# Interleaving the first two chunks of three projections, with a later split of the rows they read

## The chip, the cores and the metric

The kernel runs on one core of a Trainium2 chip. The metric is device time in microseconds of one execution. Five engines of the core work from their own instruction streams and wait for each other through semaphores: TensorE (PE, matmuls; its weight loads are listed as PEld), VectorE (DVE), ScalarE (ACT), GpSimd (POOL) and SyncE (SP, which here only issues loads). DMA queues move data beside them.

## The reference

Two layers of a decoder trunk over 256 tokens of width 2048, batch 1. What matters here is the frame around the mixers, cut to:

```python
for i in range(DEPTH):                       # DEPTH = 2
    hn = rmsnorm(h, e_norm[j] if i % 2 == 0 else o_norm[j])
    ...                                      # u = hn @ w_in; mixer (HGRN2 + RG-LRU, or mLSTM)
    mix = y @ w_out                          # output projection, 2048 x 2048
    h = h + mix
    pl = rmsnorm(p[i].astype(h.dtype) @ ple_w[i], ple_norm[i])
    h = h + jax.nn.sigmoid(h @ ple_gate_w[i]) * pl     # the gate, 2048 x 2048
return rmsnorm(h, final_norm)
```

So after each output projection the gate needs the whole new `h` as its contraction, and after the first gate the second layer's input projections (queries and keys, values `v`, output gate, `z`) need the whole `h` again.

## The kernel before

Every product is in float32, taken as three products of a high and a low part (`whi`, `wlo` of the weights, two halves of a tile `ahl` of the activations). The weights stream from memory: `load_weights` (L116 on) loads tiles of 128x1024 (`raw`), ACT casts the high part (L130) and DVE subtracts it for the low part (L131). `whi` and `wlo` have four buffers each, `raw` five, and a call of `load_weights` takes two of each.

`project_tok` (L190 on) makes a chunk: 512 output columns for 256 tokens, in two PSUM accumulators `mm`, one for each half of the tokens. It goes through four quarters of the contraction. A quarter loads its weights and issues 24 matmuls: for each token half and each of four 128-row steps, one matmul each at L205, L206 and L207. Midway in a quarter it calls `pump`, which moves every waiting side job (a Python generator in a "lane") by one step. A job's step places its instructions at that point of the program, behind the last cast and the last matmul recorded; the casts have a higher priority. The framework's scheduler then orders each engine's stream by these places, priorities and its own estimates. Every engine runs its stream in order.

The activations of a projection are needed with features on the partitions, but an output projection or a gate leaves tokens there. `to_features` (L353 on) turns one chunk round: DVE transposes blocks of 32 (L358), POOL writes the tile `w` to memory (`dfe`, `dfg` or `dfo`, L485 in `across`) and reads it back in four pieces as `r` (L488); after three steps of waiting, ACT and DVE split `r` into the `ahl` tiles (L374 and L376, or L366 and `split_act`, L145 and L146, where a gain is applied). Call the whole a hop. In the first gate, `more` then issues the gate sums (L907, on PE) two steps later, on the same `r`.

`out_proj` makes four chunks, adds each to the hidden state (L397) and starts its hop (lane "fe" in the first layer, "fo" in the second). `ple_gate`, the first gate, makes four chunks from those rows; each ends in a tanh (L410), two DVE operations (L411, L412), a square sum (L263) and a new hop (lane "fg"). The values of the second layer (`ov`) are four chunks from the "fg" rows. The last gate (`g1`, L1139 on) is three chunks from the "fo" rows, then two half chunks in another form (L1156 to L1158).

The first chunk of each of these three projections gets `before = ready(act, lane)`: ahead of quarter kq it steps the lane's job until chunk kq's rows are in `act`. So quarter 4 of a projection's first chunk reads what the last chunk before it has only just produced.

Of the kernel before, what the change touches and what calls it, by code (L numbers as in the profile page):

```python
# [11 lines left out]
F32 = mybir.dt.float32  # L12
# [7 lines left out]
P = 128  # L20
T = 256
D = 2048
KT = D // P
# [20 lines left out]
def trunk(ctx: ExitStack, tc: tile.TileContext, a, out):  # L44
    nc = tc.nc
    v, s, gp, te, sy = nc.vector, nc.scalar, nc.gpsimd, nc.tensor, nc.sync
# [6 lines left out]
    pm = ctx.enter_context(tc.tile_pool(name="pm", bufs=3, space=PSUM))  # L53
    px = ctx.enter_context(tc.tile_pool(name="px", bufs=3, space=PSUM))
# [6 lines left out]
    last = {}  # L61
# [12 lines left out]
    def pump():  # L74
        with ExitStack() as behind:
            for ins in last.values():
                behind.enter_context(tc.issue_after(ins))
            for lane in list(lanes):
                step(lane)
# [36 lines left out]
    def load_weights(src, pieces=1, queues=(sy,)):  # L116
        parts = []
        for hf in range(2):
            raw = wp.tile([P, 1024], F32, name="raw", tag="raw", bufs=5)
            hi = wp.tile([P, 1024], F32R, name="whi", tag="whi")  # L120
            lo = wp.tile([P, 1024], F32R, name="wlo", tag="wlo")
            n = 1024 // pieces
            for c in range(0, 1024, n):
                r, h, l = (x[:, c:c + n] for x in (raw, hi, lo))
                queues[(hf * 1024 + c) // n % len(queues)].dma_start(out=r, in_=src[:, hf * 1024 + c:hf * 1024 + c + n])
                with ExitStack() as order:
                    order.enter_context(tc.high_priority(offset=400))
                    if pieces > 1:
                        order.enter_context(tc.issue_after(last["split"]))
                    last["act"] = s.copy(h, r).ins  # L130
                    last["dve"] = v.tensor_tensor(out=l, in0=r, in1=h.bitcast(F32), op=ALU.subtract).ins  # L131
            parts.append((hi, lo))
            pieces = 1
        return parts
# [52 lines left out]
    def tokens(x, k, hf):  # L187
        return x[:, k, hf * P:(hf + 1) * P]

    def project_tok(w, j, act, before=None):  # L190

        ps = [pm.tile([P, 512], F32, name="mm", tag="mm") for _ in range(2)]
        for kq in range(4):
            if before is not None:
                before(kq)
            parts = load_weights(w[4 * j + kq])
            for hf in range(2):
                for kk in range(4):
                    k = kq * 4 + kk
                    hi, lo = parts[kk // 2]  # L200
                    c = (kk % 2) * 512
                    ah, al, _ = act[k // 2]
                    xh, xl = (tokens(x, k % 2, hf) for x in (ah, al))
                    wh, wl = hi[:, c:c + 512], lo[:, c:c + 512]
                    te.matmul(ps[hf], xh, wh, start=(k == 0), stop=False)  # L205
                    te.matmul(ps[hf], xh, wl, start=False, stop=False)  # L206
                    last["pe"] = te.matmul(ps[hf], xl, wh, start=False, stop=(k == KT - 1)).ins  # L207
                if hf == 0:
                    pump()
        return ps  # L210

    def newton(y, t, r, yh):
        v.tensor_scalar(t.bitcast(I32), y.bitcast(I32), 1, None, op0=ALU.logical_shift_right)
# [139 lines left out]
    def to_features(h, c, act, gain, name, more=None):  # L353

        w = room("w")
        w5 = w.rearrange("p (j c h t) -> p h c j t", j=4, c=4, h=2)
        for hf in range(2):
            v.transpose(w5[:, hf], h[:, hf].rearrange("p (c j q) -> p c j q", c=4, j=4))  # L358
        r = room("r")
        yield from across(w, r, f"d{name}{c}")  # L360
        r5 = r.rearrange("p (i c h t) -> p c h i t", i=4, c=4, h=2)
        for b in range(2):
            if gain:
                x = tp.tile([P, 512], F32, name="xr", tag="hn", bufs=3)
                for k in range(2):
                    s.activation(x[:, k * T:(k + 1) * T].rearrange("p (h i t) -> p h i t", h=2, i=4), r5[:, 2 * b + k],  # L366
                                 AF.Copy, scale=pc(gain, 4 * c + 2 * b + k))
                act[2 * c + b] = split_act(x, "h")
            else:
                hi, lo, both = act_pair()  # L370
                for k in range(2):
                    src = r5[:, 2 * b + k]
                    hk, lk = (x[:, k].rearrange("p (h i t) -> p h i t", h=2, i=4) for x in (hi, lo))
                    s.copy(hk, src)  # L374
                    for hf in range(2):
                        v.tensor_tensor(out=lk[:, hf], in0=src[:, hf], in1=hk[:, hf].bitcast(F32), op=ALU.subtract)  # L376
                act[2 * c + b] = (hi, lo, both)
        if more is not None:
            yield
            yield  # L380
            more(c, r5)

    def ready(act, lane):

        def before(kq):
            while 2 * kq + 1 not in act:
                step(f"{lane}{kq}")
        return before
# [13 lines left out]
    def ple_gate(hq, w, act, pls, rp, hss, gain, lane, before, more):  # L402

        nxt = {}
        for c in range(4):
            ps = project_tok(w, c, act, None if c else before)
            for hf in range(2):
                th = tp.tile([P, 512], F32, name="th", tag="th")
                h = hq[c][:, hf]
                s.activation(th, ps[hf], AF.Tanh, scale=0.5)  # L410
                v.scalar_tensor_tensor(th, th, 1.0, pls[c][hf], op0=ALU.add, op1=ALU.mult)  # L411
                v.scalar_tensor_tensor(h, th, rp[:, hf:hf + 1], h, op0=ALU.mult, op1=ALU.add)  # L412
            start(f"{lane}{c}", to_features(hq[c], c, nxt, gain, lane, more))
            step(f"{lane}{c}")
            for hf in range(2):
                squared(hq[c][:, hf], hss[:, c, hf:hf + 1])
        return nxt
# [21 lines left out]
    acth = []  # L439
# [39 lines left out]
        v.tensor_scalar(norm["rth"], norm["rt"], 0.5, None, op0=ALU.mult)  # L479
        yield  # L480

    def across(w, r, name):

        d = dr.tile([P, 1024], F32, name=name)
        gp.dma_start(out=d, in_=w)  # L485
        to = r.rearrange("p (i n) -> p i n", i=4)
        for j in range(4):
            last["hop"] = gp.dma_start(out=to[32 * j:32 * j + 32],  # L488
                                       in_=d.rearrange("(i q) (j n) -> j q i n", i=4, j=4)[j]).ins
        for _ in range(3):  # L490
            yield

    def feature_major(u, gain, first, y, room):

        w = room("w")
        w5 = w.rearrange("p (j c h t) -> p h c j t", j=4, c=4, h=2)
        for hf in range(2):
            v.transpose(w5[:, hf], u[:, hf].rearrange("p (c j q) -> p c j q", c=4, j=4))  # L498
        r = room("r")
        yield from across(w, r, f"du{gain}{first}")  # L500
        r5 = r.rearrange("p (i c h t) -> p c h i t", i=4, c=4, h=2)
        for b in range(2):
            x = tp.tile([P, 512], F32, name="xr", tag="hn", bufs=3)
            for k in range(2):
                s.activation(x[:, k * T:(k + 1) * T].rearrange("p (h i t) -> p h i t", h=2, i=4), r5[:, 2 * b + k],
                             AF.Copy, scale=pc(gain, first + 2 * b + k))
            y[first // 2 + b] = split_act(x, "y")
# [387 lines left out]
    act = out_proj(hq, a["eo"], y, "fe")  # L895
# [30 lines left out]
    with tc.tile_pool(name="m1", bufs=2) as m1:  # L926
# [18 lines left out]

        VW = 257
        vts = []
        for j in range(4):
            psv = project_tok(a["ov"], j, acth, None if j else ready(acth, "fg"))
            if j == 0:  # L950
                drain("norm")
            vt = m1.tile([P, 2, 2, VW], F32, name="vt", tag="vt", bufs=6)
            gp.memset(vt[:, :, :, 256:VW], 1.0)
            for hf in range(2):
                s.activation(vt[:, hf, :, 0:256], psv[hf].rearrange("p (i e) -> p i e", i=2), AF.Copy,
                             scale=norm["rt"][:, hf:hf + 1])
            vts.append(vt)
# [178 lines left out]
                v.scalar_tensor_tensor(sq, pl, 1.0, pl, op0=ALU.mult, op1=ALU.mult, accum_out=o)  # L1136

        warm = tp.tile([P, 1], F32, name="warm", tag="warm", bufs=1)
        for g in range(3):  # L1139
            ps = project_tok(a["g1"], g, act, None if g else ready(act, "fo"))  # L1140
            for hf in range(2):
                pl = pls[g][hf]
                gated(g, ps[hf], hq[g][:, hf], pl, hf)
                gp.tensor_tensor(out=pl, in0=pl, in1=fnr[g // 2][:, (g % 2) * 512:(g % 2 + 1) * 512], op=ALU.mult)
# [178 lines left out]
```

## Time and profile before

| | us |
|---|---|
| median of 3 runs | 1086.08 |
| lowest and highest run | 1077.75, 1087.19 |
| the profiled execution's own time | 1081.47 |
| its span, first to last instruction | 1079.6 |
| PE busy in it | 1047.7 |
| DVE busy, ACT busy | 724.8, 586.5 |
| mean granted PE clock | 0.989 |

The profile is of one execution. A busy time is the sum of an engine's instructions; matmuls are pipelined, so a busy PE need not be at its peak. Idle time before an instruction is put down to what released it. The granted clock is a share of full speed. In a timeline row stand the start, the duration, the engine and line, the operation, and in brackets the engine's idle time before it and the releaser.

### The profile page before, as it was taken

What the parts mean: (1) busy time and instruction counts of PE and PEld (TensorE: products, weight loads), DVE (VectorE), ACT (ScalarE), POOL (GpSimd) and SP (SyncE); (2) the same over time, 40 slices, a digit from 0 to 9 for tenths busy, and PEclk for the clock granted to TensorE, in tenths of its full rate; (3) what the DMA queues carried; (4) which work ended last, traced back from release to release, by engine and by line L of the source; (5) the groups of instructions that cost most, each with busy time, mean ns of one, the idle gap of its engine ahead of it and who ended that gap; (6) DMA issues with size and microseconds to landing.
All of it is one profiled execution on the core that took longest, in us unless ns stands there. A gap on an engine that the chain in (4) does not pass through costs nothing.

```text
span 1079.6 us, 15164 instructions
## 1 busy us (share of the span) xinstructions
PE 1047.7 (97%) x5614; PEld 878.7 (81%) x5614; DVE 724.8 (67%) x1075; ACT 586.5 (54%) x885; POOL 140.5 (13%) x166
## 2 busy tenths in 40 slices
PE   8999999999999997999899999999999999998996
PEld 6888888888888776888588888888888888887886
DVE  7756887997776654766344787765446776755666
ACT  7675545879554433655444666654445565444453
POOL 0001232511206111111000000000001113211111
PEclk9999999999999998999899999999999999999999
DMA  9755453545877666766555544445557775887452
GB/s 359 285 200 195 160 190 128 199 159 185 291 240 252 208 202 194 233 220 220 170 197 190 181 155 159 158 160 200 191 193 231 247 260 191 289 233 242 163 188 79
DMA packets 63098, 221.21 MB, mean 205 GB/s; under 512 B 7728, under 2 KB 9008, under 8 KB 63024
## 3 DMA queue, kind: packets, MB, share of 16 engines
q1 hardware_dynamic: 55440, 196.64, 54.9%
q0 software_dynamic: 7152, 23.07, 6.9%
q8 instruction: 44, 0.72, 0.3%
q10 hardware_dynamic: 432, 0.52, 0.1%
q14 instruction: 30, 0.25, 0.1%
HBM read 209.20 MB, written 11.01 MB: 204 GB/s over the span
## 4 chain that ended last, share of the span: by engine, by line
PE 46%; DMA 2%; issue 2%; ACT 1%; POOL 1%; DVE 0%; ACTq 0%; POOLq 0%
PE mm L205 11%; PE mm L206 11%; PE mm L207 11%; PE mm L161 5%; PE mm L167 3%; DMA r<-dfg 1%; PE mm L1158 1%; PE mm L1157 1%; PE mm L1156 1%; PE nu L1038 1%; DMA r<-ducn 1%; DMA r<-dfo 1%; POOL r L488 1%; DMA ducn<-w 0%; ACT whi L130 0%
## 5 line engine op out<-in xcount | busy, mean ns | idle before, releaser
L131 DVE TENSOR_TENSOR wlo<-raw,whi 128x1024 fp32r<-128x1024 f32 (+1 forms) x363 | 444.5, 1242 | 252.6 <-ACT whi L130 218.4
L130 ACT CAST whi<-raw 128x1024 fp32r<-128x1024 f32 (+1 forms) x363 | 376.6, 1043 | 328.3 <-PE mm L207 238.9
L205 PE MATMUL mm<-whi,ahl 128*128 128x512 f32 x992 | 391.8, 395 | 15.2 <-ACT ahl L374 9.1
L206 PE MATMUL mm<-wlo,ahl 128*128 128x512 f32 x992 | 389.5, 393 | 2.6 <-DVE wlo L131 2.6
L207 PE MATMUL mm<-whi,ahl 128*128 128x512 f32 x992 | 387.3, 391 | 0.0
L205 PEld LDWEIGHTS mm<-whi,ahl 128*128 128x128 f32 x992 | 188.1, 190 | 57.7 <-ACT ahl L374 9.7
L206 PEld LDWEIGHTS mm<-wlo,ahl 128*128 128x128 f32 x992 | 188.4, 190 | 43.1 <-DVE wlo L131 4.1
L207 PEld LDWEIGHTS mm<-whi,ahl 128*128 128x128 f32 x992 | 187.4, 189 | 39.2
L161 PE MATMUL mm<-ahl,whi 128*128 128x512 f32 x768 | 183.1, 390 | 0.0
L161 PEld LDWEIGHTS mm<-ahl,whi 128*128 128x128 f32 x768 | 141.3, 188 | 27.5
L167 PE MATMUL mm<-ahl,wlo 128*128 128x256 f32 x768 | 102.1, 286 | 0.0
L167 PEld LDWEIGHTS mm<-ahl,wlo 128*128 128x128 f32 x768 | 97.2, 191 | 3.6 <-issue 0.4
L485 POOL DMA_DIRECT2D ducn<-w x3 | 1.7, 561 | 337.5 <-DVE w L498 337.5
L173 ACT COPY sm<-mm 128x256 f32<-128x256 f32 x48 | 17.6, 366 | 30.6 <-PE mm L167 30.5
L376 DVE TENSOR_TENSOR ahl<-r,ahl 128x128 fp32r<-128x128 f32 x64 | 15.0, 288 | 19.3 <-ACT ahl L374 19.3
L374 ACT CAST ahl<-r 128x256 fp32r<-128x256 f32 x32 | 11.4, 402 | 26.4 <-DMA r<-dfe 20.4
L939 DVE SCALAR_TENSOR_TENSOR qk<-mg,prm,qk 128x255 f32<-128x255 f32 (+2 forms) x48 | 21.1, 478 | 5.0 <-ACT qk L936 4.7
L174 DVE TENSOR_TENSOR mg<-mm,sm 128x256 f32<-128x256 f32 x48 | 19.9, 416 | 0.1
L315 PE MATMUL mm<-whi,ahl 128*128 128x512 f32 x32 | 13.8, 431 | 5.5 <-ACT whi L130 5.2
L1157 PE MATMUL mm<-wlo,ahl 128*128 128x256 f32 x64 | 18.1, 283 | 0.0
L1158 PE MATMUL mm<-whi,ahl 128*128 128x256 f32 x64 | 18.1, 283 | 0.0
L1156 PE MATMUL mm<-whi,ahl 128*128 128x256 f32 x64 | 18.1, 283 | 0.0
(284 smaller groups left out, 795.6 us busy)
## 6 DMA issues: line engine op xcount, KB each, us to landing
raw<-in_ew_dram SPq DMA_DIRECT2D x64, 512.0 KB, 4.1
raw<-in_g_dram SPq DMA_DIRECT2D x56, 512.0 KB, 4.8
raw<-in_eo_dram SPq DMA_DIRECT2D x32, 512.0 KB, 5.0
raw<-in_ov_dram SPq DMA_DIRECT2D x32, 512.0 KB, 3.9
raw<-in_oqk_dram SPq DMA_DIRECT2D x32, 512.0 KB, 4.0
raw<-in_oog_dram SPq DMA_DIRECT2D x32, 512.0 KB, 3.9
raw<-in_oz_dram SPq DMA_DIRECT2D x32, 512.0 KB, 3.9
raw<-in_oo_dram SPq DMA_DIRECT2D x32, 512.0 KB, 4.5
```

What stands on the lines that cost most here:

```text
L130: last["act"] = s.copy(h, r).ins
L131: last["dve"] = v.tensor_tensor(out=l, in0=r, in1=h.bitcast(F32), op=ALU.subtract).ins
L161: last["pe"] = te.matmul(ps, parts[k // 8][0][:, c:c + P], act[k // 2][2][:, (k % 2) * 512:(k % 2 + 1) * 512], start=(k == 0), stop=False).ins
L167: last["pe"] = te.matmul(ps[:, T:2 * T], parts[k // 8][1][:, c:c + P], act[k // 2][0][:, k % 2], start=False, stop=(k == KT - 1)).ins
L174: v.tensor_tensor(out=dst, in0=ps[:, 0:T], in1=small, op=ALU.add)
L205: te.matmul(ps[hf], xh, wh, start=(k == 0), stop=False)
L206: te.matmul(ps[hf], xh, wl, start=False, stop=False)
L207: last["pe"] = te.matmul(ps[hf], xl, wh, start=False, stop=(k == KT - 1)).ins
L939: v.scalar_tensor_tensor(dst[:, sh:T], pi[:, 0:T - sh], pc("ccw", k * 16 + b), dst[:, sh:T], op0=ALU.mult, op1=ALU.add)
L1156: te.matmul(ps[hf], xh, wh, start=(k == 0), stop=False)
L1157: te.matmul(ps[hf], xh, wl, start=False, stop=False)
L1158: last["pe"] = te.matmul(ps[hf], xl, wh, start=False, stop=(k == KT - 1)).ins
```

## The change

`project_tok`'s inner part becomes `quarter_tok`. A new `project_two` makes the first two chunks of a projection together: quarters 1, 2, 3 of the first, quarters 1, 2, 3 of the second, then the first's quarter 4 and the second's. The second chunk's accumulators come from another PSUM pool (`px`, tag `mx`). `chunks` yields the first two from there and the others as before. The first gate, the values and the last gate use it. In `to_features` the wait after the reads is five steps instead of three, and `more` follows after one step instead of two, so the gate sums stand one step later than before. `feature_major`, the same turn for the mixers' outputs, keeps three.

```diff
+    def project_two(w, act, before):
+
+        ps = [[pool.tile([P, 512], F32, name=name, tag=name) for _ in range(2)]
+              for pool, name in ((pm, "mm"), (px, "mx"))]
+        for j, kq in ((0, 0), (0, 1), (0, 2), (1, 0), (1, 1), (1, 2), (0, 3), (1, 3)):
+            before(kq)
+            quarter_tok(w, j, kq, act, ps[j])
+            if kq == 3:
+                yield ps[j]
+
+    def chunks(w, n, act, before):
+        yield from project_two(w, act, before)
+        for j in range(2, n):
+            yield project_tok(w, j, act)
...
-        yield from across(w, r, f"d{name}{c}")
+        yield from across(w, r, f"d{name}{c}", 5)
...
         if more is not None:
             yield
-            yield
             more(c, r5)
...
-        for c in range(4):
-            ps = project_tok(w, c, act, None if c else before)
+        for c, ps in enumerate(chunks(w, 4, act, before)):
...
-        for j in range(4):
-            psv = project_tok(a["ov"], j, acth, None if j else ready(acth, "fg"))
+        for j, psv in enumerate(chunks(a["ov"], 4, acth, ready(acth, "fg"))):
...
-        for g in range(3):
-            ps = project_tok(a["g1"], g, act, None if g else ready(act, "fo"))
+        for g, ps in enumerate(chunks(a["g1"], 3, act, ready(act, "fo"))):
...
-        for _ in range(3):
+        for _ in range(lag):
             yield
```

Below, rows of the order in which an engine's instructions stand. Numbers behind names tell tiles apart, and lines of the kernel after are up to 20 higher (L205 to L207 become L225 to L227, L374 becomes L393). First PE before, in the first gate, from the end of the first chunk's quarter 3 (`mm_4021`, weights `whi_4101`) on; `ahl_4118` holds rows of the last hop, `mm_4202` is the second chunk:

```order
L207 MATMUL mm_4021<-whi_4101,ahl_3947 128x512
L205 MATMUL mm_4202<-whi_4205,ahl_3595 128x512
L205 MATMUL mm_4020<-whi_4145,ahl_4118 128x512
L206 MATMUL mm_4020<-wlo_4146,ahl_4118 128x512
L205 MATMUL mm_4021<-whi_4145,ahl_4118 128x512
L206 MATMUL mm_4021<-wlo_4146,ahl_4118 128x512
L206 MATMUL mm_4202<-wlo_4206,ahl_3595 128x512
L207 MATMUL mm_4020<-whi_4145,ahl_4118 128x512
```

One matmul of the second chunk stands ahead of the first that reads `ahl_4118`. PE after, at the same place and then at the end of the second chunk's quarter 3 (`mx_4009`, `whi_4225`); the last hop's rows are `ahl_4192` here:

```order
L227 MATMUL mm_4007<-whi_4103,ahl_4041 128x512
L225 MATMUL mx_4008<-whi_4133,ahl_3682 128x512
L226 MATMUL mx_4008<-wlo_4134,ahl_3682 128x512
...
L227 MATMUL mx_4009<-whi_4225,ahl_4041 128x512
L225 MATMUL mm_4006<-whi_4255,ahl_4192 128x512
L226 MATMUL mm_4006<-wlo_4256,ahl_4192 128x512
```

The second chunk's three quarters, 72 matmuls, have moved ahead of the first matmul that reads the last hop's rows. Now ACT before, at the split of the last hop (`r_4007`); `whi_4145` and `whi_4151` are the first chunk's quarter 4, `whi_4205` and `whi_4211` the second chunk's quarter 1:

```order
L130 COPY whi_4145<-raw_4144 128x1024
L130 COPY whi_4151<-raw_4150 128x1024
L130 COPY whi_4205<-raw_4204 128x1024
L374 COPY ahl_4118<-r_4007 128x256 x2
L130 COPY whi_4211<-raw_4210 128x1024
L374 COPY ahl_4125<-r_4007 128x256 x2
```

And ACT after (`r_3993` is the last hop; `whi_4169` and `whi_4175` are the second chunk's quarter 2, `whi_4219` its quarter 3):

```order
L130 COPY whi_4169<-raw_4168 128x1024
L130 COPY whi_4175<-raw_4174 128x1024
L393 COPY ahl_4192<-r_3993 128x256 x2
L393 COPY ahl_4199<-r_3993 128x256 x2
L130 COPY whi_4219<-raw_4218 128x1024
```

Counted in quarters from the gate's start, the splits stood behind the first cast of the fifth, and now stand behind the second cast of the fifth; no cast stands between them any more, and the second cast of quarter 5 has moved ahead. The earlier hops' splits have moved by one cast in the same way.

More of the change, by code (lines that the diff above doesn't have):

```diff
@@ L195, in project_tok, with quarter_tok @@
                 before(kq)
[L196 to L209, printed above, removed]
-        return ps
+            quarter_tok(w, j, kq, act, ps)
+        return ps
+    def project_two(w, act, before):
[10 more added lines that the diff above has]
+            yield project_tok(w, j, act)
+    def quarter_tok(w, j, kq, act, ps):
+        parts = load_weights(w[4 * j + kq])
+        for hf in range(2):
+            for kk in range(4):
+                k = kq * 4 + kk
+                hi, lo = parts[kk // 2]
+                c = (kk % 2) * 512
+                ah, al, _ = act[k // 2]
+                xh, xl = (tokens(x, k % 2, hf) for x in (ah, al))
+                wh, wl = hi[:, c:c + 512], lo[:, c:c + 512]
+                te.matmul(ps[hf], xh, wh, start=(k == 0), stop=False)
+                te.matmul(ps[hf], xh, wl, start=False, stop=False)
+                last["pe"] = te.matmul(ps[hf], xl, wh, start=False, stop=(k == KT - 1)).ins
+            if hf == 0:
+                pump()
     def newton(y, t, r, yh):
@@ L480, in spread_norm, with across @@
         yield
-    def across(w, r, name):
+    def across(w, r, name, lag):
         d = dr.tile([P, 1024], F32, name=name)
@@ L499, in feature_major @@
         r = room("r")
-        yield from across(w, r, f"du{gain}{first}")
+        yield from across(w, r, f"du{gain}{first}", 3)
         r5 = r.rearrange("p (i c h t) -> p c h i t", i=4, c=4, h=2)
```

## The prediction

> **What bounds the kernel now.** The page comes first: who is busy, and for how much of the span.
>
> ```profile
> span 1079.6 us, 15164 instructions
> PE 1047.7 (97%) x5614; PEld 878.7 (81%) x5614; DVE 724.8 (67%) x1075; ACT 586.5 (54%) x885; POOL 140.5 (13%) x166
> ```
>
> TensorE (PE) is the bound. A schedule can win only what PE is not busy (1079.6 - 1047.7 = 31.9 us) and what it loses while its clock is low. The waits of all engines say who makes it idle (engine, line, what it waited for: us in total, times, longest).
>
> ```profile
> ACT ahl L374 <- DMA r<-dfe: 20.4, 4, 7.3
> ...
> PE mm L205 <- ACT ahl L374: 9.1, 2, 5.9
> ...
> PE mm L205 <- ACT whi L130: 6.1, 2, 4.2
> ACT ahl L374 <- DMA r<-dfo: 6.0, 4, 3.3
> ```
>
> PE waits for rows that a transposing hop has just brought (ahl), or for weight casts (whi) that stand on ACT behind the wait for such a hop. The windows view places this (length, busy time of PE, PEld, DVE, ACT, POOL, then PE's granted clock); I cut it at the three places where a gated or value projection begins, and around the low clock.
>
> ```profile
> 370.00:430.00 60.00, 50.82 (x206) 40.59 (x205) 30.08 (x50) 21.96 (x31) 5.48 (x10) 0.91 0.65 196
> 375.00:385.00 10.00, 9.49 (x42) 7.86 (x43) 8.51 (x15) 4.87 (x5) 0.56 (x1) 1.00 0.60 182
> 399.90:403.30 3.40, 2.79 (x7) 2.23 (x8) 3.40 (x9) 1.82 (x2) 0.00 (x0) 0.51 0.47 142
> 420.40:427.20 6.80, 4.15 (x10) 3.28 (x11) 2.93 (x9) 2.27 (x5) 0.00 (x0) 0.50 0.29 82
> 510.00:530.00 20.00, 14.61 (x52) 10.89 (x52) 7.41 (x14) 6.71 (x12) 2.13 (x4) 0.83 0.63 181
> 519.40:526.20 6.80, 4.58 (x10) 3.33 (x11) 2.61 (x3) 3.79 (x7) 0.00 (x0) 0.50 0.58 211
> 540.00:600.00 60.00, 60.00 (x273) 49.94 (x272) 27.63 (x24) 28.32 (x30) 0.00 (x0) 1.00 0.60 196
> 990.00:1000.00 10.00, 6.80 (x25) 5.23 (x24) 4.11 (x8) 3.33 (x6) 0.62 (x2) 0.86 0.74 209
> 997.20:1000.70 3.50, 3.34 (x8) 2.69 (x9) 2.79 (x9) 1.98 (x5) 0.00 (x0) 0.51 0.17 68
> ```
>
> Idle: 60.00 - 50.82 = 9.2 us around the first gate, 5.4 at the values, 3.2 at the last gate; 17.8 of the 31.9. After each stall the clock is at half for 3.4 to 6.8 us, and half of the busy time there is lost: 1.4 + 2.1 us, 2.3 us, 1.7 us. At 540 to 600 us PE is full at clock 1.00. So the places cost 12.7, 7.7 and 4.9 us. The gate sums (L907), one set a chunk, check the middle one.
>
> ```profile
> 477.49 0.64 PE L907 MATMUL mx<-r,wg 128*32 128x256 f32 x8
> ...
> 500.05 0.64 PE L907 MATMUL mx<-r,wg 128*32 128x256 f32 x8
> ...
> 531.48 0.64 PE L907 MATMUL mx<-r,wg 128*32 128x256 f32 x8
> ```
>
> The first two are 22.56 us apart: one undisturbed chunk of 96 matmuls and its sums. The next two are 31.43 us apart with the same work and two small matmuls more, which I estimate at no more than the eight sums' 0.64: 8.2 to 8.9 us lost; I take 8.4 for the 7.7. Together 12.7 + 8.4 + 4.9 = 26.0 us.
>
> **What the change does to the first gate (12.7 us).** The timeline of ACT, then of DVE and POOL, around the last chunk of the output projection; a bracket is the idle time before a row, and its releaser.
>
> ```profile
> 389.22 1.05 ACT L130 CAST whi<-raw 128x1024 fp32r<-128x1024 f32 x1 [3.02 <-PE mm L207]
> 397.55 0.71 ACT L374 CAST ahl<-r 128x256 fp32r<-128x256 f32 x2 [7.28 <-DMA r<-dfe]
> 398.16 1.04 ACT L130 CAST whi<-raw 128x1024 fp32r<-128x1024 f32 x1
> ...
> 422.59 0.71 ACT L374 CAST ahl<-r 128x256 fp32r<-128x256 f32 x2 [5.99 <-DMA r<-dfe]
> ```
>
> ```profile
> 402.61 1.18 DVE L131 TENSOR_TENSOR wlo<-raw,whi 128x1024 fp32r<-128x1024 f32 x1
> 403.71 0.68 DVE L397 TENSOR_TENSOR hq<-mm,hq 128x512 f32<-128x512 f32 x1
> ...
> 406.44 0.56 POOL L485 DMA_DIRECT2D dfe<-w  x1 [16.19 <-DVE w L358]
> 413.10 2.18 POOL L488 DMA_DIRECT2D r<-dfe  x4 [6.09 <-ACT whi L130]
> ```
>
> A quarter (24 matmuls) takes 22.56 us less the 0.64 of sums, over four: about 5.45 us. The cast at 389.22 got its buffer after the 18th matmul of a quarter (a half-quarter's tile is last read there), so that quarter ended 1.36 us later, at 390.6, and the next, the projection's last, at 396.0. Call that G, the gate's start.
>
> Before, PE has three quarters (16.4 us) of work after G that need no row of the last hop. The last add (L397, 403.71) is 7.7 us after G, and from it to the landed rows (422.59) are 18.9 us, 26.6 us after G in all: PE starves. After, six quarters (32.7 us) come first, so the rows themselves are in time by some 4 us even if the hop gains nothing, and the 5.9 us wait goes.
>
> What is late next is ACT. The splits now stand behind the fifth quarter's second cast, and quarter 6's casts behind the splits. That second cast has its buffer at G+16.4, so ACT arrives at G+17.4 and waits for the hop: 5.5 to 9.2 us, none of it PE's own so long as quarter 6's first tile is ready at its start, G+27.3. It needs, after the landing, four splits (1.4 us, two rows of 0.71), a cast (1.05) and its low part (1.18): 3.6 us. With the old landing that is G+30.2, 2.9 us late. But the landing should move: the step of five puts the next projection's cast (398.16) and its low part ahead of the splits, and these stood between the previous chunk's rows and the next add on DVE. That shortens the way from rows to add by about 1.2 us a chunk, and the lateness that adds up over three chunks (7.7 us) to some 4 us; the landing is then G+23, the tile ready at G+26.6, in time by 0.7. Remaining stall: 0 to 2.9 us; I take 0. The 2.7 us at 397 (a cast behind a split) goes by the same move. Stake: -12.7, upper end -12.7 + 2.9 + 1.7 of clock.
>
> **Values (8.4 us).** ACT splits the gate's last hop.
>
> ```profile
> 519.66 0.51 ACT L366 ACTIVATE xr<-r,prm 128x256 f32<-128x256 f32 x1 [5.41 <-DMA r<-dfg]
> ...
> 522.87 0.62 ACT L145 CAST ahl<-xr 128x512 fp32r<-128x512 f32 x1
> ```
>
> The sums at 500.05 stand 12 matmuls (2.7 us) behind the projection's start, 497.3. The rows land at 519.66, 22.4 us after it, and could be 24 if the two short gate chunks ahead crowd DVE. Rows are needed after six quarters, 33 us: in time. Quarter 6's first tile: landing + 2.8 us of splits (522.87 + 0.62 - 519.66 = 3.8, less a cast that stood in between) + 1.05 + 1.18, that is 27.4 to 29.0 after the start, against 27.3 + 0.6 of sums + 0.4 = 28.3. A stall of 0 to 0.7 us, or 1 with what queues behind; I take 0.5.
>
> **Last gate (4.9 us).** The two rows: the end of the last quarter of its output projection as ACT's cast sees it, and the landing.
>
> ```profile
> 977.60 1.05 ACT L130 CAST whi<-raw 128x1024 fp32r<-128x1024 f32 x1 [0.30 <-DVE ahl L376]
> ...
> 996.91 0.71 ACT L374 CAST ahl<-r 128x256 fp32r<-128x256 f32 x2 [3.29 <-DMA r<-dfo]
> ```
>
> 19.3 us plus 3.6 is 22.9, well under 27.3. All 4.9 us go.
>
> **The tail of chunks 1 and 2.** The two now end 5.45 us apart, not 21.8, and each leaves gate work on DVE.
>
> ```profile
> 429.90 0.69 DVE L411 SCALAR_TENSOR_TENSOR th<-th,pl 128x512 f32<-128x512 f32 x1 [3.38 <-ACT th L410]
> 430.63 0.75 DVE L412 SCALAR_TENSOR_TENSOR hq<-th,rp,hq 128x512 f32<-128x512 f32 x1
> ```
>
> With a transpose of 0.7 us that is 2.1 us a half, 8.6 us for two chunks, beside 2.4 us of low parts a quarter; three quarters hold 16.3, and casts run two quarters ahead. So DVE covers it. Their two hops follow each other on POOL: the second's write waits for the first's four reads to be issued, 6.09 + 2.18 us. Its rows are wanted only by the values, over 30 us on. ACT, however, waits for the first of these hops with chunk 4's first casts behind it. Chunk 1 ends after quarter 7, chunk 4 starts five quarters on, 27.3 us; by the values' hop the rows land 22.4 to 24 us after the chunk's end and the tile is ready 5.0 later, 27.4 to 29.0: a stall of 0 to 1.7 us; I take 0.5. The sums moved one step are the same matmuls: nothing.
>
> Sum: -12.7 - 8.4 - 4.9 + 0.5 + 0.5 = -25.0 us on the profiled execution of 1081.47: 1056.5. That execution is 0.4% under the median shown (1086.08, of 1077.75 to 1087.19). I take the spread to be mostly these same stalls, so that little of it remains, and say 1057.
>
> The row at 399.90 has half clock after a stall of 1.9 us for a cast (6.1 less 4.2) and one under 1 us for a low part; the last gate's 3.2 us did the same, while the 0.5 us at 375 to 385 left the clock at 1.00. [...]
>
> **Rivals.** (1) *The split step does less than its number.* The steps are five instead of three, but on ACT the splits stand one cast later, not four. If the hop is no earlier for it, quarter 6's casts come late at both long boundaries: 2.9 + 1.7 at the gate, the same 1.7 of clock and 1 at the values, and the 397 stall stays in part (2). 1056.5 + 9.3 = 1066. For: ACT's waits of 20.4 us in four; against: at the last gate, where the same slot was used, they are 6.0 in four. (2) *The waits spread: slower.* Every hop holds ACT in line, with casts behind it. There are twelve such hops. If each cost PE what the one at 397 did, 2.7 us and 1.4 of clock, that is 49 us, less 26.0: 1104. It decides when hops take over some 22 us from add to rows instead of 19, since ACT's slot is fixed at about 4 us ahead of a chunk's end; the two bunched hops would start it. Against: at the last gate's three earlier hops ACT waited 2.7 us in all (6.0 less 3.3). [...] (4) *The stalls are not worth their length*: something else, such as the weight loads' DMA, takes the place at once, and only half of the idle time is won with the clock dips left, 9 us: 1072.
>
> **How the numbers follow.** Forecast 0.72, (1) 0.14, (4) and mixtures within 1% 0.09, (2) 0.03, (3) 0.02. A measurement of this kernel tells about 1%, 10.9 us, from no change. The likeliest case spans 1051 (lowest run shown less 26.0) to 1063 (bounds 4.6, 1 and 1.7 late instead of 0, 0.5 and 0.5, on 1056.5); rival (1) lies at 1066 and up to 0.4% above, 1070. Range 1050 to 1069, which leaves out (2), (3), most of (4): under 0.2. Faster by over 1%: 0.72 + 0.14 + 0.01 = 0.87; same 0.08; slower 0.05.
>
> **What would show it.** PE idle from the projection's end through eight quarters under 2 us at each place; PE's waits for ahl of L374 gone; clock 1.00 through all three; ACT waiting 4 to 7 us for dfe once, with no PE wait behind it; the gate sums 22.6 us apart where chunks are whole. Wrong if PE waits for whi in the sixth quarter, or half-clock windows stand inside the pairs.

## The result and the profile after

The changed kernel takes 1054.69 us (median of 4 runs, 1053.82 to 1056.46), the kernel before 1083.36 us (median of 4, 1077.75 to 1087.19): a ratio of 0.9741, 95% interval 0.9691 to 0.9792. Ratios, here and below, are taken over the runs that lie within 1.5% of the fastest of the same kernel. The profiled executions are 1054.51 and 1081.47 us, 26.96 us apart; 1057 us had been forecast, in a range of 1050 to 1069. The spread of the runs has shrunk from 0.9% to 0.25%.

The head of the page of the changed kernel, and its row of TensorE's clock over 40 slices:

```profile
span 1052.7 us, 15167 instructions
PE 1038.7 (99%) x5614; PEld 874.2 (83%) x5614; DVE 728.2 (69%) x1075; ACT 588.2 (56%) x885; POOL 138.9 (13%) x166
PEclk9999999999999999999999999999999999999999
```

PE's idle time has fallen from 31.9 to 14.0 us (1052.7 - 1038.7), and the same 5614 matmuls are busy 9.0 us less (1047.7 - 1038.7): of the span's 26.9 us, 17.9 were idle time and 9.0 were clock. The waits of PE are down to two rows, one of them at the start of the program, and ACT's wait for dfe is still long:

```profile
PE mm L334 <- ACT whi L130: 5.2, 1, 5.2
PE mm L225 <- DVE hq L415: 0.2, 1, 0.2
...
ACT ahl L393 <- DMA r<-dfe: 16.7, 4, 6.0
```

The windows view (length, busy time of PE, PEld, DVE, ACT and POOL, then PE's clock) at the first gate, the values and the last gate:

```profile
370.00:430.00 60.00, 59.84 (x263) 49.03 (x262) 35.39 (x55) 26.37 (x34) 5.49 (x10) 1.00 0.73 224
490.00:520.00 30.00, 30.00 (x143) 23.68 (x142) 16.70 (x29) 14.84 (x21) 2.74 (x5) 1.00 0.68 218
960.00:1000.00 40.00, 40.00 (x178) 33.13 (x177) 23.60 (x28) 19.67 (x26) 4.60 (x6) 1.00 0.69 223
```

All three stalls are gone, and no half-clock window is left. Two gate sums of whole chunks are now 492.68 - 470.12 = 22.56 us apart, the undisturbed distance:

```profile
470.12 0.64 PE L924 MATMUL mx<-r,wg 128*32 128x256 f32 x8
492.68 0.64 PE L924 MATMUL mx<-r,wg 128*32 128x256 f32 x8
```

ACT's timeline around the first gate shows how near it was:

```profile
388.57 1.05 ACT L130 CAST whi<-raw 128x1024 fp32r<-128x1024 f32 x1 [3.02 <-PE mm L227]
...
396.42 1.33 ACT L393 CAST ahl<-r 128x256 fp32r<-128x256 f32 x4 [5.43 <-DMA r<-dfe]
397.65 2.00 ACT L130 CAST whi<-raw 128x1024 fp32r<-128x1024 f32 x2
...
419.39 1.33 ACT L393 CAST ahl<-r 128x256 fp32r<-128x256 f32 x4 [6.03 <-DMA r<-dfe]
420.62 3.90 ACT L130 CAST whi<-raw 128x1024 fp32r<-128x1024 f32 x4
```

By the way of the prediction the gate starts at G = 388.57 + 1.36 + 5.44 = 395.4. The last hop's rows are split at 419.39, G + 24.0 (forecast G + 23); behind four splits stand four casts that all had been waiting. The first of them is quarter 6's and is done at about 421.7, G + 26.3; with its low part it is ready about when PE wants it, at G + 27.3. ACT still waits 6 us there, and PE notices nothing. POOL's rows of the same hops (the write to DRAM), and DVE's rows between them:

```profile
379.77 0.56 POOL L502 DMA_DIRECT2D dfe<-w  x1 [14.27 <-DVE w L377]
403.54 0.56 POOL L502 DMA_DIRECT2D dfe<-w  x1 [14.45 <-DVE w L377]
```

```profile
396.86 0.70 DVE L395 TENSOR_TENSOR ahl<-r,ahl 128x128 fp32r<-128x128 f32 x3 [4.61 <-ACT ahl L393]
397.47 0.68 DVE L415 TENSOR_TENSOR hq<-mm,hq 128x512 f32<-128x512 f32 x1
...
400.81 0.68 DVE L415 TENSOR_TENSOR hq<-mm,hq 128x512 f32<-128x512 f32 x1
...
402.54 0.71 DVE L377 STREAM_TRANSPOSE w<-hq 128x512 f32<-128x512 f32 x1
```

This shows a loop that the prediction used only in part. The add of a chunk (L415) stands on DVE behind the low parts of the previous chunk's rows (L395), and these wait for the splits, which wait for the previous hop. So a late hop delays the next hop's write by as much. From the split at 396.42 to the next write at 403.54 is 7.12 us; call this the way. In the kernel before, by the rows shown in the prediction, it was 406.44 - 397.55 = 8.89 us. A chunk takes PE 4 x 5.45 = 21.8 us; a hop, from its write to the split of its rows, took 396.42 - 379.77 = 16.65 us here. Hop and way together are then 23.8 us, more than PE's 21.8, and these rows come 2 us later than those of the chunk before. In the kernel before, the third write stands here:

```profile
381.44 0.56 POOL L485 DMA_DIRECT2D dfe<-w  x1 [15.60 <-DVE w L358]
```

Its hop took 397.55 - 381.44 = 16.11 us; with 8.89 that makes 25.0, and one chunk earlier it was 15.50 + 8.91 = 24.4. So there the rows fell back by 2.6 and 3.2 us a chunk.

### The profile page after: what moved, and what is told of

It is laid out like the page before. It is cut to its first block, busy times and chain, and to the rows that moved or that the text cites. A ratio compares the mean times of both kernels' runs of the same rounds, so it can differ in the third digit from the quotient of the medians.

```text
span 1052.7 us, 15167 instructions
## 1 busy us (share of the span) xinstructions
PE 1038.7 (99%) x5614; PEld 874.2 (83%) x5614; DVE 728.2 (69%) x1075; ACT 588.2 (56%) x885; POOL 138.9 (13%) x166
## 4 chain that ended last, share of the span: by engine, by line
PE 92%; DMA 3%; issue 2%; DVE 1%; ACT 1%; POOL 0%; ACTq 0%; DVEq 0%; POOLq 0%
PE mm L225 17%; PE mm L226 17%; PE mm L227 17%; PE mm L161 17%; PE mm L167 9%; PE mx L225 2%; PE mx L227 2%; PE mx L226 2%; DMA dfe<-w 2%; DMA r<-dfe 1%; PE mm L334 1%; PE mm L335 1%; PE mm L336 1%; PE mm L1173 1%; PE mm L1172 1%
## 5 line engine op out<-in xcount | busy, mean ns | idle before, releaser
L225 PE MATMUL mm<-whi,ahl 128*128 128x512 f32 x896 | 350.5, 391 | 0.2 <-DVE hq L415 0.2
L226 PE MATMUL mm<-wlo,ahl 128*128 128x512 f32 x896 | 348.8, 389 | 0.0
L227 PE MATMUL mm<-whi,ahl 128*128 128x512 f32 x896 | 348.7, 389 | 0.0
L225 PEld LDWEIGHTS mm<-whi,ahl 128*128 128x128 f32 x896 | 168.2, 188 | 36.6 <-issue 0.8
L227 PEld LDWEIGHTS mm<-whi,ahl 128*128 128x128 f32 x896 | 168.2, 188 | 35.3
L226 PEld LDWEIGHTS mm<-wlo,ahl 128*128 128x128 f32 x896 | 168.2, 188 | 34.7 <-DVE wlo L131 0.3
L225 PE MATMUL mx<-whi,ahl 128*128 128x512 f32 x96 | 37.7, 392 | 0.0
L227 PE MATMUL mx<-whi,ahl 128*128 128x512 f32 x96 | 37.4, 389 | 0.0
L226 PE MATMUL mx<-wlo,ahl 128*128 128x512 f32 x96 | 37.4, 389 | 0.0
L173 ACT COPY sm<-mm 128x256 f32<-128x256 f32 x48 | 17.6, 366 | 31.9 <-PE mm L167 31.8
L395 DVE TENSOR_TENSOR ahl<-r,ahl 128x128 fp32r<-128x128 f32 x64 | 14.4, 281 | 12.4 <-ACT ahl L393 12.4
L225 PEld LDWEIGHTS mx<-whi,ahl 128*128 128x128 f32 x96 | 18.0, 188 | 4.1 <-issue 0.4
L227 PEld LDWEIGHTS mx<-whi,ahl 128*128 128x128 f32 x96 | 18.0, 188 | 3.8
L226 PEld LDWEIGHTS mx<-wlo,ahl 128*128 128x128 f32 x96 | 18.0, 188 | 3.7
```

Source lines behind the costliest of these rows:

```text
L173: s.copy(small, ps[:, T:2 * T])
```

## The experiments

Times stand beside runs of the kernel before in the same series; its median was 1087.7, 1084.35 and 1080.23 us in the three series, so ratios say more than differences of medians.

**The halves alone.** Of the changed kernel, *inter3* keeps the interleaving at all three places, with the split where it was:

```diff
-        yield from across(w, r, f"d{name}{c}", 5)
+        yield from across(w, r, f"d{name}{c}", 3)
...
         if more is not None:
             yield
+            yield
```

> The interleaving at all three places, with the splits at three steps as before. Theory A (two separate causes: the interleaving takes away the wait for the last hop's rows, the later split takes away the casts that queue behind a split on ACT and brings the landing from 26.6 to 23 or 24 us after the gate's start): values and last gate gain in full, 8.4 + 4.9 us; at the first gate the 2.7 us stall and its 1.4 us of clock near 397 stay, and since quarter 5's second cast then stands between the splits of a hop that lands 26.6 us after the gate's start, PE waits about 5 us for it in quarter 5 with some 2 us of clock; in all 13 to 15 us faster than before. Theory B (the interleaving does it all, the split's step nothing): 25 to 28 us faster, as the full change, and no PE wait for whi near 397. Theory C (the split's step does most): under 6 us faster.

*lag5* is the reverse, the kernel before with the later split alone:

```diff
-        yield from across(w, r, f"d{name}{c}")
+        yield from across(w, r, f"d{name}{c}", 5)
...
         if more is not None:
             yield
-            yield
...
```

> The splits five steps on, no interleaving. Theory A: the 2.7 us stall near 397 and its half clock (1.4 us) go, and 0.6 us at 375; the last hop lands some 2.6 us earlier, so the wait for its rows at the first gate falls from 5.9 to about 3.3 us; the stalls at the values (5.4 us) and at the last gate (3.2 us) stay: 6 to 8 us faster than before. Theory B: within 1.5 us of before, the stall near 397 still there. Theory C: over 20 us faster.

Measured: inter3 1061.94 us, ratio 0.9785 (0.9732 to 0.9837); lag5 1063.13 us, ratio 0.9791 (0.9741 to 0.9842). Theory A expected 13 to 15 and 6 to 8 us. The ratios, on some 1085 us, make it 23 and 23, where the whole change makes 28. Theory A falls on both; C is right for lag5 alone and B nearly for inter3. Each half by itself takes most of the gain, and the gains don't add: 23 + 23 against 28.

What is left of the stalls in lag5, in PE's timeline at the first and the last gate, and its window at the values:

```profile
414.47 0.50 PE L205 MATMUL mm<-whi,ahl 128*128 128x512 f32 x1 [1.79 <-ACT ahl L374]
...
980.66 0.50 PE L205 MATMUL mm<-whi,ahl 128*128 128x512 f32 x1 [1.48 <-ACT ahl L374]
```

```profile
500.00:530.00 30.00, 29.24 (x133) 23.13 (x132) 14.45 (x15) 15.32 (x21) 0.00 (x0) 1.00 0.62 195
```

In this execution 5.9 us have become 1.79, 3.2 have become 1.48, and the 5.4 at the values 0.76, without any interleaving. ACT's and POOL's timelines of lag5 say why:

```profile
371.81 1.33 ACT L374 CAST ahl<-r 128x256 fp32r<-128x256 f32 x4 [1.84 <-DMA r<-dfe]
...
393.25 1.33 ACT L374 CAST ahl<-r 128x256 fp32r<-128x256 f32 x4 [1.51 <-DMA r<-dfe]
...
414.01 0.71 ACT L374 CAST ahl<-r 128x256 fp32r<-128x256 f32 x2 [1.89 <-DMA r<-dfe]
```

```profile
378.94 0.56 POOL L484 DMA_DIRECT2D dfe<-w  x1 [13.67 <-DVE w L358]
...
400.37 0.56 POOL L484 DMA_DIRECT2D dfe<-w  x1 [13.31 <-DVE w L358]
```

Split to next write is 7.13 and 7.12 us (378.94 - 371.81, 400.37 - 393.25), as in the changed kernel. The hop between them took 393.25 - 378.94 = 14.31 us; with the way to the next write 21.4, just inside 21.8. So lateness doesn't grow. Not all of this is the later split's doing: the hops of this execution were also shorter than in the profile of the kernel before (14.59, 14.31 and 13.64 us against 15.50, 16.11 and 16.15). Counted from the first gate's first matmul (395.82 before, 395.92 in lag5), the last write is issued 6.2 us earlier and the rows come 8.7 us earlier. At the last gate (977.40 and 962.42) the write is only 0.7 us earlier; 1.0 us of the 1.7 gained there is a shorter hop. In inter3 the way has its old length:

```profile
370.66 0.71 ACT L393 CAST ahl<-r 128x256 fp32r<-128x256 f32 x2 [3.01 <-DMA r<-dfe]
```

```profile
379.57 0.56 POOL L503 DMA_DIRECT2D dfe<-w  x1 [14.78 <-DVE w L377]
```

379.57 - 370.66 = 8.91 us: rows come late as before, and the interleaving covers them at the boundary. The stall that theory A expected in its fifth quarter (5 us) did not come; the last hop took 14.03 us here, against 16.15 in the kernel before. PE's waits in inter3, besides the one at the start, are these:

```profile
PE mm L225 <- ACT whi L130: 0.8, 1, 0.8
PE mm L226 <- DVE wlo L131: 0.8, 1, 0.8
PE mx L226 <- DVE wlo L131: 0.8, 1, 0.8
PE mx L225 <- ACT whi L130: 0.7, 1, 0.7
```

**The interleaving at one place, with the later split.** *only_fe* interleaves at the first gate alone, *only_g1* at the last gate alone; the other callers take the chunks one after the other:

```diff
-    def chunks(w, n, act, before):
-        yield from project_two(w, act, before)
-        for j in range(2, n):
-            yield project_tok(w, j, act)
+    def chunks(w, n, act, before, two=True):
+        if two:
+            yield from project_two(w, act, before)
+        for j in range(2 if two else 0, n):
+            yield project_tok(w, j, act, None if j else before)
...
```

> Five steps, interleaved at the first gate only. Theory A, if the parts add: 12 to 13 us faster than before; values and last gate keep their stalls of 5.4 and 3.2 us with half clock behind them. Theory B: the same 12 to 13, so this run alone does not part A from B. Theory D (a stall that is taken away at one place comes back at the next, so that parts do not add): under 10 us faster, with the stall at the values longer than 5.4 us.

> Five steps, interleaved at the last gate only. Theory A, if the parts add: what the later split alone gains (6 to 8 us) and 4.9 us at the last gate: 11 to 13 us faster than before, 5 us more than the later split alone. Theory B: 5 us faster than before in all. Theory D: no more than the later split alone gains, with a new stall of 3 us or more behind the last gate.

Measured: only_fe 1060.88 us, 0.9771 (0.9721 to 0.9822), some 25 us against the 12 to 13 of theories A and B, and no longer stall at the values (0.76 us), so D falls too. only_g1 1067.40 us, 0.9829 (0.9761 to 0.9898), with runs from 1057.56 to 1071.48: 18 to 19 us, more than any of its three theories allowed and, within the intervals, no more than lag5. It gives no figure for the last gate: up to there it issues lag5's instructions in lag5's order, and yet its profile has three times lag5's stall at the first gate:

```profile
416.95 0.79 PE L226 MATMUL mm<-whi,ahl 128*128 128x512 f32 x1 [5.36 <-ACT ahl L394]
```

```profile
401.48 0.56 POOL L503 DMA_DIRECT2D dfe<-w  x1 [12.92 <-DVE w L378]
```

```profile
416.49 0.71 ACT L394 CAST ahl<-r 128x256 fp32r<-128x256 f32 x2 [5.46 <-DMA r<-dfe]
```

Here the last hop took 15.0 us (416.49 - 401.48), in lag5 13.6 (414.01 - 400.37). What a hop takes differs between executions, and without cover at the boundary the longer one ended in the stall of 5.36 us here. The 23 us of the later split alone are therefore no fixed figure: at the first gate this execution, with the same order, keeps most of the stall.

**A longer hop.** The write of each of the twelve hops is issued twice, in four kernels: before, the two halves, and the change.

```diff
         gp.dma_start(out=d, in_=w)
+        if name[:2] != "du":
+            gp.dma_start(out=d, in_=w)
```

> The kernel before, with the write of each of the twelve feature hops (dfe, dfg, dfo) issued twice, which lengthens a hop by about one write, 5 to 6.5 us; the result is the same. Theory E (one cause: a hop of 11 to 17 us from write to rows runs against a slot that ACT's order fixes; rows that come late hold ACT, that delays the next chunk's add, and so the next hop; each half of the change widens the slot by itself): the hops that are late already cost these 6 us in full, the others 2 to 5, with clock on top: 45 to 80 us slower than before. Theory F (the change gains by something other than the hops' slot): about as much slower, within 10 us, as the changed kernel with the same longer hop.

> The later split alone, with the same longer hop. Theory E: the slot is wider by one cast, about 4 us, at every hop, but the last hop of each boundary keeps only three quarters of cover: about 6 us at each of the three last hops and 1 to 3 at the others, with clock: 20 to 45 us slower than the later split alone, 1083 to 1108 us. Theory F: as much slower, within 10 us, as the changed kernel with the same longer hop.

> The interleaving alone, with the same longer hop. Theory E: the last hops have cover to spare for their rows, but the hops in the midst of a projection keep the old slot and cost 3 to 6 us each: 25 to 50 us slower than the interleaving alone, 1087 to 1112 us, with PE waiting for whi behind the splits. Theory F: as much slower, within 10 us, as the changed kernel with the same longer hop.

> The changed kernel with the same longer hop. Theory E: its slack at the first gate is nearly used (ACT, free again at 397.65, has only 0.25 us of idle time before the next cast but one), so dfe's hops cost 3 to 6 us each; dfg's and dfo's have not held ACT at all and cost 0 to 2 each: 15 to 30 us slower than the changed kernel, 1070 to 1085 us; the full change then gains 45 us or more over the kernel before with the same hop. Theory F: the gain stays near 28 us.

| with the longer hop | median, us | ratio to before (95%) | against the same kernel with its own hop, medians |
|---|---|---|---|
| before | 1112.76 | 1.0279 (1.0198 to 1.0360) | +28.4 |
| later split | 1116.16 | 1.0315 (1.0230 to 1.0400) | +53.0 |
| interleaving | 1090.90 | 1.0075 (1.0033 to 1.0118) | +29.0 |
| both | 1094.48 | 1.0118 (1.0036 to 1.0200) | +39.8 |

Theory E is right for inter3_2x alone (25 to 50 expected); before slows less than its 45 to 80, the later split and the full change more than their 20 to 45 and 15 to 30. The full change gains 18 us here, not 45 or more, and not F's 28 either. The later split, worth 23 us alone with the old hop, shows no gain with the longer one (1116.16 against 1112.76), but this pair does not test it. The second write also changed the order in which the framework's scheduler placed the splits. In the kernel before, two splits stand behind one cast and two behind the next; in before2x all four stand together behind the second of them, as in lag5_2x. ACT's rows of before2x and of lag5_2x at the third hop:

```profile
403.48 1.33 ACT L374 CAST ahl<-r 128x256 fp32r<-128x256 f32 x4 [5.89 <-DMA r<-dfe]
```

```profile
405.36 1.32 ACT L374 CAST ahl<-r 128x256 fp32r<-128x256 f32 x4 [9.84 <-DMA r<-dfe]
```

From the start to the middle of the first gate, ACT's order is the same in both, and so it is in inter3_2x and after2x. So, as far as the splits' place on ACT goes, the table compares two kernels rather than four, one interleaved and one not (DVE's order still differs a little within each pair); at the first and the last gate all have the later place of the splits. DVE of lag5_2x, in the last chunk of the output projection, and PE's wait that follows from it:

```profile
405.80 0.29 DVE L376 TENSOR_TENSOR ahl<-r,ahl 128x128 fp32r<-128x128 f32 x1 [9.02 <-ACT ahl L374]
406.01 0.68 DVE L396 TENSOR_TENSOR hq<-mm,hq 128x512 f32<-128x512 f32 x1
```

```profile
PE mm L205 <- DVE hq L396: 9.8, 3, 4.2
```

Now the add waits behind the late rows' low part, and PE waits for the accumulator that the add should have emptied: a wait that the kernel before does not have (before2x has it once, for 1.0 us). The loop is closed in all four kernels, and hop and way are longer than a chunk. In before2x they are 403.48 - 385.68 = 17.8 and 410.13 - 403.48 = 6.65 us, in all 24.5 against 21.8; at the same hop they make 27.6 us in lag5_2x, 25.5 in inter3_2x and 26.7 in after2x. So in before2x a chunk takes 24.45 us from write to write (385.68 to 410.13). The hop itself grew by 2 to 4 us in before2x, not by the 5 to 6.5 expected. The interleaving still helps, by 22 us in either pair; that it does so because it acts at the boundary, once per place, is argued and not shown. POOL's rows of before2x are:

```profile
385.68 0.56 POOL L485 DMA_DIRECT2D dfe<-w  x1 [10.71 <-DVE w L358]
...
410.13 0.56 POOL L485 DMA_DIRECT2D dfe<-w  x1 [12.68 <-DVE w L358]
```

**No hop in the loop.** Theory G came out of this, and its test takes the hop out: chunks 1 to 3 read back chunk 0's rows, written long before, so that no split waits for its own chunk's write.

```diff
+    first_d = {}
...
         gp.dma_start(out=d, in_=w)
+        if name[:2] != "du":
+            d = first_d.setdefault(name[:3], d)
```

> The kernel before, in which the hops of chunks 1 to 3 at the first gate, the values and the last gate still write their rows but read back those of chunk 0, so that no split waits for its own chunk's write (the features of three quarters are wrong); the order on ACT moves a little with it. Theory G (a closed loop: a chunk's write can't be issued before the previous chunk's rows have landed, 8.9 us later at three steps and 7.1 us at five; with hops of 13 to 16 us this exceeds the 21.8 us that PE needs for a chunk, and the excess adds up until PE starves): without the loop all of its stalls go, 1050 to 1058 us, as the changed kernel. Theory H (part of the gain is of another origin, such as the order of the matmuls or the clock under them): it stays 10 us or more above the changed kernel.

> The changed kernel with the same edit: the hops of chunks 1 to 3 read back the rows of chunk 0. Theory G: nothing is left for the hops to cost there, so within 3 us of the changed kernel, and within 5 us of the kernel before with the same edit. Theory H: the two kernels with this edit lie 10 us or more apart.

Measured: before_old 1056.00 us, 0.9799 (0.9747 to 0.9851); after_old 1056.26 us, 0.9803 (0.9742 to 0.9864). The kernel before, neither interleaved nor split later in its code, is as fast as the changed one once its hops can't be late. Its page:

```profile
span 1053.0 us, 15168 instructions
PE 1037.9 (99%) x5614; PEld 873.9 (83%) x5614; DVE 729.0 (69%) x1075; ACT 588.3 (56%) x885; POOL 140.4 (13%) x166
```

PE is busy for 1037.9 us and idle for 15.1, against 1038.7 and 14.0 in the changed kernel. H falls, as far as the 0.5% of these intervals tells. One reservation: with the hop out of the way the order moved too, and from the second hop of a projection on the splits stand three casts earlier on ACT than in the kernel before. What the run shows is that without late hops neither the interleaving nor a later split is needed for 1056 us. It takes away the loop and the wait at the boundary together, so it doesn't say how they share the gain.

**The change again, and one step more.** *after_again* is the changed kernel; *lag6* splits six steps on:

```diff
-        yield from across(w, r, f"d{name}{c}", 5)
+        yield from across(w, r, f"d{name}{c}", 6)
```

> The changed kernel once more, for a measurement beside the other runs and a second profile. Theory G: 1053 to 1057 us; splits of a chunk and write of the next 7.1 us apart at the first gate whatever the hop took; PE without a stall over 1 us at the three places unless a hop takes over 17 us.

> The changed kernel with the split six steps on instead of five: on ACT the splits then stand behind quarter 6's two casts. Theory G: the casts at stake behind the last hop's splits are then those of the quarter that needs the rows, so a late hop costs less; as PE has hardly a stall left at the three places, the time stays within 3 us of the changed kernel. A rival: the later split delays the low parts and the rows themselves, and PE waits for ahl by 1 to 3 us at the first gate, 1057 to 1062 us.

Measured: after_again 1055.02 us, 0.9796 (0.9752 to 0.9841; one run of six at 1062.65), no stall over 0.8 us and split to next write again 7.12 us. Its instructions stand in the same order as in the first profile, but its hops were shorter. The third one, on POOL and on ACT:

```profile
378.61 0.56 POOL L502 DMA_DIRECT2D dfe<-w  x1 [13.55 <-DVE w L377]
```

```profile
393.21 1.33 ACT L393 CAST ahl<-r 128x256 fp32r<-128x256 f32 x4 [1.71 <-DMA r<-dfe]
```

Hop and way are 14.60 + 7.12 = 21.7 us here, just under a chunk, and ACT's waits for the last three hops stay at 1.76, 1.71 and 1.94 us. In the first profile, with 16.65 us and more than a chunk, they grow: 3.42, 5.43, 6.03. One kernel thus shows the loop on both sides of its bound, and both executions take 1054 us, since the interleaving covers either.

lag6 1061.00 us, 0.9832 (0.9782 to 0.9882), 1053.55 to 1066.62. Neither G (within 3 us) nor its rival fits the cause: in its profile (1061.89) PE has no stall at the three places, and ACT no wait for any of the twelve hops. What it has is a stall of 3.13 us at 859 us, at another hop (ducn, which feature_major issues, and whose step the edit leaves at three), with half clock behind it. Around the stall the order of ACT and DVE is that of the changed kernel; only_fe, split five steps on, has a stall of 1.38 us at the same wait. Whether lag6 brings it or this execution had it by chance isn't settled, and no more is claimed of lag6 than that it isn't faster.

## Why the prediction was right, and where its account was not

- **The sum.** 26.0 us for the three places were forecast, less 1.0 for new stalls; the profiled executions are 26.96 us apart, 17.9 idle and 9.0 clock. Sizing the gain by the stalls and by the half-clock windows behind them was right. The two terms of 0.5 us that were set against it (the values' sixth quarter, the tail of chunks 1 and 2) did not come: PE's waits hold no row for them.
- **The first gate.** The landing was forecast at G + 23 and the sixth quarter's tile 0.7 us before its need; the profile shows G + 24.0 and nothing to spare. The remaining stall of 0 to 2.9 us was taken at 0 and is 0, in this execution without margin, so that what its hops happened to take decided it too. ACT waits 6.03 us for the last hop, inside the forecast's 5.5 to 9.2.
- **The step that failed** is "That shortens the way from rows to add by about 1.2 us a chunk", and with it the giving of all 8.4 us at the values and "All 4.9 us go" to the interleaving. The way is shorter by 8.9 - 7.1 = 1.8 us. More than that, it is part of a closed loop whose excess over a chunk adds up: 2.6 and 3.2 us a chunk ahead of the first gate, and ahead of the values 13.10 + 10.89 = 24.0 us against the 22.56 of a chunk with its sums. Ahead of the last gate there is hardly any excess (13.31 + 8.91 = 22.2 against 21.8). So the later split alone takes most of the first two stalls in lag5's execution, which the prediction's working would have put at no more than the 397 stall and a few us; the shorter hops of that execution have a part in it. The change's total is bounded by the stalls that exist, and there the two halves overlap; this is why the total came out right all the same.
- **Rival (1)**, that the split step does less than its number, went the wrong way: it does more. That the splits move by one cast on ACT and not by four is so, but one cast takes 1.8 us a chunk out of a loop that was 2.6 and 3.2 us too long.
- **Rival (2)**, that the waits spread when hops take too long, was right as a mechanism and not reached here. after2x shows it: with hops made longer, the changed kernel has seven stalls of 2 to 6 us and is 1.2% (0.4% to 2.0%) slower than the kernel before with its own hop.
- **The 0.02 under (3)** was for clock lost without a stall, by switching among four accumulators. No run shows such a loss: in the windows at the three places the changed kernel's clock is 1.00, with PE busy for 129.84 of 130 us. **Rival (4)**, stalls not worth their length: 17.9 us of idle time gone and another 9.0 of clock; they are worth half as much again.
- **The spread.** That the spread of the kernel before is mostly these stalls fits: 1077 to 1087 us without cover, 1054 to 1056 in the first series with it; in the later series they are 1068 to 1102 and 1054 to 1063. The run at 1062.65 was not profiled, so that what it met is open.

## What to carry to other kernels

Where a transfer's result must pass through in-order engines on its way to the next transfer's source, add up the loop (here hop 13 to 17 us, plus 7 or 9 us on ACT and DVE) and set it against the time of one pass (21.8 us): over it, at 23.8 us in the changed kernel's first profile, the excess added up pass by pass and ACT's waits grew from 3.42 to 6.03 us; under it, at 21.7 us in after_again, they stayed at 1.7 to 1.9. Two remedies for the same stalls didn't add here; try each alone before keeping both. Keep the second if executions differ: a last hop of 15.0 us cost only_g1 5.36 us, and one of 15.85 us cost the changed kernel, with its cover at the boundary, nothing. And where a scheduler orders the instructions, look at the order again after every edit: a second write, meant only to lengthen a hop, moved the splits as well. Size a stall with the clock behind it, not by its length alone: here 17.9 us of idle time came with 9.0 of clock.

## What the runs showed of the hardware

**The same hop differs in time.** The third hop of dfe took 16.65 us in one execution of the changed kernel and 14.60 in another (after_again), with every engine's instructions in the same order; in lag5 it took 14.31. No run tells what the difference comes from.

**A stall of 1.79 us was followed by a lowered clock, one of 2.09 us was not.** The windows behind stalls in lag5 (1.79 us at 412.68, then 1.48 us at 979.18):

```profile
414.50:417.90 3.40, 3.40 (x10) 2.68 (x11) 2.84 (x9) 1.78 (x4) 0.00 (x0) 0.67 0.41 147
417.90:421.30 3.40, 3.40 (x14) 2.72 (x13) 0.35 (x2) 1.01 (x2) 0.00 (x0) 0.83 0.50 154
...
980.70:984.10 3.40, 3.40 (x15) 2.79 (x16) 2.84 (x9) 1.78 (x4) 0.00 (x0) 1.00 0.47 164
```

and in lag6, behind the 3.13 us at 859:

```profile
862.40:866.40 4.00, 3.99 (x9) 2.89 (x10) 4.00 (x6) 3.71 (x5) 0.00 (x0) 0.50 0.25 86
```

Behind 1.48 us the clock stayed at 1.00, behind 1.79 us it was 0.67 and 0.83 (means of the next two windows), and behind 3.13 us 0.50 over 4 us. With 0.76 us of idle time it was 1.00 (lag5's window at the values, above); in inter3 0.83 and 0.76 us with 0.5 us of work between them, at 396.48, were followed by this:

```profile
398.60:402.00 3.40, 3.40 (x11) 2.68 (x12) 3.40 (x9) 1.16 (x2) 0.00 (x0) 0.69 0.45 154
```

while 0.65 and 0.76 us at 981.87 in the same run cost nothing (1.00 in the window behind), nor did 1.38 and 1.06 us with 1.7 us of work between them in only_fe (858.13 and 861.19, 1.00 in every window behind). And in lag5_2x a stall of 2.09 us, with one of 0.76 behind it, cost nothing either:

```profile
985.95 0.50 PE L205 MATMUL mm<-whi,ahl 128*128 128x512 f32 x1 [2.09 <-ACT whi L130]
```

```profile
985.94:989.34 3.40, 2.56 (x9) 1.59 (x10) 3.40 (x5) 2.80 (x3) 0.00 (x0) 1.00 0.32 83
```

So a lowered clock is seen here after a single stall as short as 1.79 us, but not after each of that length. Behind the longer ones it was near half: 0.54 behind the 5.36 us of only_g1 (416.90 to 420.30), and in the kernel before 0.50, 0.50 and 0.51 in the 3.4 us behind 5.90, 4.17 and 3.20 us (423.05, 521.16, 997.36). Behind the 5.18 us at the start of the changed kernel the view gives 1.00 (5.00 to 8.40), though the matmuls from 6.56 on start 0.43 us apart, against 0.23 at 462.66 to 463.56. What else decides about the shorter ones, no run here shows.
